# A fixed order for TensorE in the RWKV scans: small products grouped by shape in each hop, three units of the output projection moved to the end

## Chip, cores and metric

The kernel runs on one core of a Trainium2 chip. The metric is the device time of one execution in microseconds; it is compared as the median of several runs.

## The reference

One layer of a hybrid backbone over 640 tokens (512 latent, 128 context) of 2048 channels: RMS norm with adaLN modulation, an input projection, a bidirectional RWKV-7 time mixing of 16 heads on one half of the channels and a gated MLP on the other, an output projection, then a SwiGLU channel mixer and a last norm. The change touches the RWKV scan and the output projection behind it:

```python
def _delta_scan(r, w, k, v, aa, bb, s0, reverse):
    def step(S, inp):
        r_t, w_t, k_t, v_t, a_t, b_t = inp
        sa = jnp.einsum('bhvk,bhk->bhv', S, a_t)
        S = S * w_t[:, :, None, :] + sa[..., None] * b_t[:, :, None, :] + v_t[..., None] * k_t[:, :, None, :]
        return S, jnp.einsum('bhvk,bhk->bhv', S, r_t)
    s_fin, ys = lax.scan(step, s0, xs, reverse=reverse)
...
    for d in range(2):
        ...
        y, s_fin = _delta_scan(rh, decay, kd, vh, -kk, kk * heads(a),
                               s0[:, d].astype(F32), reverse=(d == 1))
        out = out + _group_norm(y, lp['gn_w'], lp['gn_b']) \
            + jnp.sum(rh * kd * lp['r_k'], axis=-1, keepdims=True) * vh
    o = (out.reshape(B, T, D_A) * gate).astype(dtype)
...
    x = x + g1 * (jnp.concatenate([o_a, o_b], axis=-1) @ lp['w_out'])
```

The scans run over the context alone from a zero state (its last state is an output) and over the latent tokens from a given state, in both directions.

## The kernel before

The 640 tokens are cut into ten chunks of 64: eight latent (`LATC`), two of context (`CTXC`). Sixteen heads make eight pairs (`NPAIR`); a pair holds its two heads in the two halves of the 128 partitions, and both directions d side by side. An earlier stage has worked out for each pair, direction and chunk a record of 576 columns (`REC`) and stored it in device memory (`d_S`); the scan stage loads them (`load_next`, L1041 to L1047, one record for both directions, eight buffers).

The scan stage begins at L1014. `recur(p)` (L1062) runs two chains of one pair: latent, eight steps, and context, two steps. A step has three phases, and the generator gives the word back after each:

- **w**: four products w_ps = (part of the record) x (state ST), 64 rows by 64 columns (L1117); VectorE adds a part of the record to make W (L1122). In the same phase `outputs` writes what the step before left over: y_ps is the sum of four 64x64 products with the old state (`states`, L1083) and four of 128 rows by 64 columns (`chunk`, L1088); ScalarE copies it to Y with its row sums (L1102), and the next record is loaded.
- **u**: four 64x64 products u_ps (L1132), copied back into the record by VectorE (L1135) and ScalarE (L1136).
- **s**: VectorE scales the old state to SG (L1150), four 128x64 products s_ps (L1153), and VectorE makes the new state SN = s_ps x decay + SG (L1159; L1157 where there is no old state). SN is the ST of the next step.

`swap` (L1053) transposes the states at the beginning and the end of a pair, again with four 64x64 products. All these operands are plain 32-bit floats, and each such product shows as two records in the trace.

When a pair has been through its steps, `finish(p)` (L1167) norms Y: GpSimd subtracts the means (L1182), ScalarE squares (L1186), VectorE sums (L1187), GpSimd takes the root (in the helper at L132) and multiplies (L1192), each once per direction. Then 64x64 products with unit matrices add the two directions (pO, L1200, the "join"), VectorE adds the bonus term (L1204), two products of 128x320 make each half of the gate (pmm, L496), VectorE multiplies (L1208), and the result goes to d_o.

Meanwhile `wout_b` (L1215) does the half of the output projection that does not depend on the scans: for two groups q of four 128-row blocks and 16 column blocks m, a unit `wout(m, q)` (L990) of two halves with four triples each: three products of 128x128 by 320 columns (L999, L1000, L1001). Its weights are loaded and split in two parts (L162 to L164), and VectorE adds each half to x1T (L1012). For q = 0 the columns of x are transposed first (pxT, L1232) and copied by ScalarE (L1233). The other half of the projection, which needs the scans' results, follows behind the stage (L1382 to L1384).

The order of the work: a loop of 117 hops (`hops`, L1247) advances each running pair by one phase; a new pair starts every 13 hops (`OFF`) and runs 26 hops, so two are under way most of the time. After each pair's phase the Mixer m3 issues some of `wout_b` by a budget (L1257), and after each hop the Mixer m2 some of `finish`. Before the loop, m3 runs eight units of the 32. Within this program order the framework's scheduler sets the order of each engine's queue by priority and its own estimate of when operands are ready; the queues are fixed when the program is compiled. PSUM has eight banks: two for w_ps, s_ps and swap, one for u_ps, two for y_ps, one shared by pO, pmm and pxT, two for the units of the projection.

Of the kernel before, what the change touches and what calls it, by code (L numbers as in the profile page):

```python
# [10 lines left out]
F32 = mybir.dt.float32  # L11
# [44 lines left out]
WTAIL = 8  # L56
OFF = 13
MB = 6
# [26 lines left out]
def flow_step(ctx: ExitStack, tc, x_prompt, x_sample, state_rwkv, c, c_ctx, w_mod, b_mod,  # L85
# [929 lines left out]
    with ExitStack() as ph:  # L1015
        rw = ph.enter_context(tc.tile_pool(name="rw", bufs=1))
        sm = ph.enter_context(tc.tile_pool(name="sm", bufs=2))
        pws = ph.enter_context(tc.tile_pool(name="pws", bufs=2, space=PSUM))
        pu = ph.enter_context(tc.tile_pool(name="pu", bufs=1, space=PSUM))
# [32 lines left out]

        def swap(src):  # L1053
            ps = pws.tile([P, 2, CH], F32, tag="ws", name="swap")
            for d in range(2):
                for h in range(2):
                    TE.matmul(ps[hsl(h), d, :], src[hsl(h), d, :], I2[hsl(h), :], start=True, stop=True)
            o = sm.tile([P, 2, CH], F32, tag="ST", name="ST", bufs=7)
            V.tensor_copy(o, ps)
            return o  # L1060

        def recur(p):  # L1062
# [7 lines left out]
            yield 1  # L1070
            late = []

            def outputs():
                if not late:
                    return


                ys = [py.tile([P, 2, CH], F32, tag=f"y{d}", name="y_ps") for d in range(2)]

                def states(e, r, ST, **kw):  # L1080
                    for d in range(2):
                        for h in range(2):
                            TE.matmul(ys[d][hsl(h), e, :], r[hsl(h), d, F_R + CH:F_R + P], ST[hsl(h), d, :], **kw)  # L1083

                def chunk(e, r, **kw):
                    for d in range(2):
                        for h in range(2):
                            TE.matmul(ys[d][hsl(h), e, :], r[:, d, F_G + CH * h:F_G + CH * h + CH],  # L1088
                                      r[:, d, F_Z + CH * h:F_Z + CH * h + CH], **kw)

                for e, (cc, r, ST) in enumerate(late):
                    if ST is None:
                        chunk(e, r, start=True, stop=True)
                    elif e == 0:
                        states(e, r, ST, start=True, stop=False)
                        chunk(e, r, start=False, stop=True)
                    else:
                        chunk(e, r, start=True, stop=False)
                        states(e, r, ST, start=False, stop=True)
                for e, (cc, r, ST) in enumerate(late):  # L1100
                    for d in range(2):
                        S.activation(u.Y[:, d, cc[d], :], ys[d][:, e, :], AF.Copy, accum_out=u.ys[:, d, cc[d]:cc[d] + 1])  # L1102
                    load_next()
                late.clear()

            for step in range(len(LATC)):
                act = [c for c in chains if step < len(seqs[c[0]])]
                Ws = []
                for ctx_, ST in act:
                    r = recs[p, ctx_, step]  # L1110
# [3 lines left out]
                    w_ps = pws.tile([P, 2, CH], F32, tag="ws", name="w_ps")  # L1114
                    for d in range(2):
                        for h in range(2):
                            TE.matmul(w_ps[osl(h), d, :], r[hsl(h), d, F_R:F_R + CH], ST[hsl(h), d, :],  # L1117
                                      start=True, stop=True)
                    W = sm.tile([P, 2, CH], F32, tag="W", name="W", bufs=4)
                    for h in range(2):  # L1120
                        q = osl(h)
                        V.tensor_add(W[q], w_ps[q], r[q, :, F_Z + CH * h:F_Z + CH * h + CH])  # L1122
                    Ws.append(W)
                outputs()
                yield 1
                for (ctx_, ST), W in zip(act, Ws):
                    r = recs[p, ctx_, step]
                    ups = pu.tile([P, 2, CH], F32, tag="u", name="u_ps")
                    for d in range(2):
                        for h in range(2):  # L1130
                            q = osl(h)
                            TE.matmul(ups[q, d, :], r[q, d, F_T:F_T + CH],  # L1132
                                      r[q, d, F_Z + CH * h:F_Z + CH * h + CH] if W is None else W[q, d, :],
                                      start=True, stop=True)
                    V.tensor_copy(r[0:64, :, F_Z + CH:F_Z + P], ups[0:64])  # L1135
                    S.copy(r[64:128, :, F_Z:F_Z + CH], ups[64:128])  # L1136
                yield 1
                for ch in act:
                    ctx_, ST = ch
                    cc = seqs[ctx_][step]  # L1140
                    r = recs.pop((p, ctx_, step))
                    late.append((cc, r, ST))
                    if step + 1 == len(seqs[ctx_]) and not ctx_:
                        continue
                    s_ps = pws.tile([P, 2, CH], F32, tag="ws", name="s_ps")
                    SN = sm.tile([P, 2, CH], F32, tag="ST", name="SN", bufs=7)
                    ge = gend[:, p].rearrange("p d c -> p (d c)")[:, flip(cc)].unsqueeze(2)
                    if ST is not None:
                        SG = sm.tile([P, 2, CH], F32, tag="SG", name="SG", bufs=4)
                        V.tensor_tensor(out=SG, in0=ST, in1=ge.to_broadcast([P, 2, CH]), op=ALU.mult)  # L1150
                    for d in range(2):
                        for h in range(2):
                            TE.matmul(s_ps[hsl(h), d, :], r[:, d, F_X + CH * h:F_X + CH * h + CH],  # L1153
                                      r[:, d, F_Z + CH * h:F_Z + CH * h + CH], start=True, stop=True)
                    for d in range(2):
                        if ST is None:
                            V.tensor_scalar_mul(SN[:, d, :], s_ps[:, d, :], ge[:, d])  # L1157
# [756 lines left out]
```

## Time and profile before

| | |
|---|---|
| median of three runs | 3405.29 us (3395.33 to 3405.65) |
| the profiled execution | 3410.02 us |
| its span | 3408.2 us |
| granted TensorE clock, mean | 0.97 |
| first w_ps of the scan | 1242.1 us |
| last copy of y_ps | 1537.8 us |

The times in the views are microseconds from the beginning of the span. PE is TensorE's products, DVE VectorE, ACT ScalarE, POOL GpSimd, SP the engine that issues most transfers. A row of the table of windows has the stretch, its length, then for each engine the busy time and the number of instructions (PE, weight loads, DVE, ACT, POOL), the granted clock, the share of the transfer engines and GB/s. A row of the groups has line, engine, operation, output and inputs, shape and number, then the busy time in us and the mean of one in ns, then the idle time ahead of it and what ended it. A row of the timeline has the start, the time until the last one ends, engine, line and number; products are pipelined, so the distance of starts is what a product holds of the queue, and its own time is longer.

### The profile page before, as it was taken

How to read it: one execution, taken by the hardware profiler on the slowest of the kernel's cores; microseconds unless marked ns; L12 is line 12 of the kernel's file. 1: busy time of each engine (PE TensorE's matmuls, PEld its weight loads, DVE VectorE, ACT ScalarE, POOL GpSimd, SP SyncE). 2: the span in 40 equal slices, each digit the busy share in tenths (PEclk: the TensorE clock that was granted, in tenths of full speed). 3: DMA queues.
4: the chain of work that ended last, by engine and by line, in shares of the span. 5: the costliest groups of instructions: out<-in, count | busy, mean ns of one | idle time of the engine just before them, and what ended most of it. 6: DMA issues, size and time to landing. Idle time of an engine off the chain costs nothing.

```text
span 3408.2 us, 72541 instructions
## 1 busy us (share of the span) xinstructions
PE 3249.5 (95%) x28216; PEld 2934.2 (86%) x28216; DVE 2411.4 (71%) x4320; ACT 1450.7 (43%) x3161; POOL 1263.0 (37%) x1112
## 2 busy tenths in 40 slices
PE   6899999999999999998899999999999999999996
PEld 3688777777877887777889999999999999999996
DVE  4547666756866766664887777777777787877787
ACT  3334443433434434333564444444444445443365
POOL 0001122111212103322336565656656555555543
PEclk8999999889999999999999999999999999999998
DMA  8766776566677677654543434344343455543553
GB/s 321 233 188 185 184 189 170 154 171 179 186 186 180 170 226 231 209 163 145 173 124 103 130 114 122 114 126 122 111 123 121 129 165 165 158 138 115 154 163 115
DMA packets 736208, 550.11 MB, mean 161 GB/s; under 512 B 140360, under 2 KB 670040, under 8 KB 727032
## 3 DMA queue, kind: packets, MB, share of 16 engines
q1 hardware_dynamic: 723544, 531.78, 52.5%
q0 software_dynamic: 9984, 13.13, 1.8%
q8 instruction: 222, 3.64, 0.4%
q14 instruction: 122, 1.00, 0.1%
q10 hardware_dynamic: 2336, 0.57, 0.1%
HBM read 436.68 MB, written 111.28 MB: 161 GB/s over the span
## 4 chain that ended last, share of the span: by engine, by line
PE 76%; DVE 11%; issue 4%; DMA 4%; POOL 2%; ACT 2%; SPq 0%; DVEq 0%; ACTq 0%; POOLq 0%
PE P L1529 15%; PE P L1527 14%; PE P L1528 14%; PE big L185 4%; PE big L187 4%; PE big L186 4%; PE pG L624 3%; PE pm L869 2%; PE big L999 2%; DMA raw<-in_w_in_dram 1%; DVE lo L1330 1%; DMA wt<-in_w_mod_dram 1%; PE big L1382 1%; PE big L1384 1%; PE pmm L496 1%
## 5 line engine op out<-in xcount | busy, mean ns | idle before, releaser
L1529 PE MATMUL P<-xo,lo 128*128 128x320 f32 x2352 | 728.1, 310 | 2.3 <-DVE lo L1330 2.2
L1527 PE MATMUL P<-xo,hi 128*128 128x320 f32 x2352 | 727.8, 309 | 1.8 <-ACT hi L1329 1.8
L1528 PE MATMUL P<-xo,hi 128*128 128x320 f32 x2352 | 727.7, 309 | 0.0
L1330 DVE TENSOR_TENSOR lo<-raw,hi 128x512 fp32r<-128x512 f32 x532 | 502.7, 948 | 179.1 <-ACT hi L1329 174.3
L1329 ACT CAST hi<-raw 128x512 fp32r<-128x512 f32 x532 | 330.7, 622 | 496.5 <-PE P L1528 395.1
L185 PE MATMUL big<-h_hi,hi 128*128 128x320 f32 x1376 | 458.2, 333 | 7.8 <-ACT h_hi L341 4.0
L1529 PEld LDWEIGHTS P<-xo,lo 128*128 128x128 f32 x2352 | 442.5, 188 | 3.0 <-DVE lo L1330 3.0
L187 PE MATMUL big<-h_hi,lo 128*128 128x320 f32 x1376 | 444.2, 323 | 0.7 <-DVE lo L164 0.7
L186 PE MATMUL big<-h_lo,hi 128*128 128x320 f32 x1376 | 443.7, 322 | 0.9 <-DVE h_lo L342 0.9
L1527 PEld LDWEIGHTS P<-xo,hi 128*128 128x128 f32 x2352 | 442.7, 188 | 2.0 <-ACT hi L1329 2.0
L1528 PEld LDWEIGHTS P<-xo,hi 128*128 128x128 f32 x2352 | 442.5, 188 | 0.0
L1440 POOL TENSOR_TENSOR raw<-raw 128x512 f32<-128x512 f32 x252 | 407.6, 1627 | 14.9 <-DVE lo L1330 3.3
L1529 PE MATMUL P<-xd,lo 128*128 128x320 f32 x1232 | 383.3, 311 | 14.1 <-DVE lo L1330 13.7
L1527 PE MATMUL P<-xd,hi 128*128 128x320 f32 x1232 | 381.8, 310 | 4.2 <-ACT hi L1329 1.9
L1528 PE MATMUL P<-xd,hi 128*128 128x320 f32 x1232 | 380.7, 309 | 0.0
L164 DVE TENSOR_TENSOR lo<-raw,hi 128x512 fp32r<-128x512 f32 x268 | 185.7, 695 | 243.1 <-ACT hi L163 217.7
L185 PEld LDWEIGHTS big<-h_hi,hi 128*128 128x128 f32 x1376 | 268.4, 195 | 84.0 <-issue 56.9
L163 ACT CAST hi<-raw 128x512 fp32r<-128x512 f32 x268 | 165.4, 619 | 292.4 <-PE big L186 143.1
L186 PEld LDWEIGHTS big<-h_lo,hi 128*128 128x128 f32 x1376 | 268.6, 195 | 17.4 <-issue 11.8
L187 PEld LDWEIGHTS big<-h_hi,lo 128*128 128x128 f32 x1376 | 268.2, 195 | 12.2 <-issue 4.8
L1329 ACT CAST hi<-rawd 128x512 fp32r<-128x512 f32 (+1 forms) x288 | 168.9, 588 | 244.6 <-PE P L1528 207.7
L1529 PEld LDWEIGHTS P<-xd,lo 128*128 128x128 f32 x1232 | 231.2, 188 | 20.4 <-DVE lo L1330 20.3
(362 smaller groups left out, 6303.3 us busy)
## 6 DMA issues: line engine op xcount, KB each, us to landing
wt<-in_w_mod_dram SPq DMA_DIRECT2D x96, 1024.0 KB
raw<-in_w_ffn_gate_dram SPq DMA_DIRECT2D x182, 256.0 KB
raw<-in_w_ffn_up_dram SPq DMA_DIRECT2D x182, 256.0 KB
rec<-d_S SPq DMA_DIRECT2D x80, 576.0 KB
raw<-in_w_in_dram SPq DMA_DIRECT2D x172, 256.0 KB
rawd<-in_w_ffn_down_dram SPq DMA_DIRECT2D x128, 256.0 KB
raw<-in_w_out_dram SPq DMA_DIRECT2D x96, 256.0 KB
xd<-d_os SPq DMA_DIRECT2D x66, 320.0 KB
```

The lines of the kernel that those rows point to most:

```text
L163: S.copy(hi, raw)
L164: V.tensor_sub(lo, raw, hi.bitcast(F32))
L185: TE.matmul(halves[hf], hi[:, k, :], h_hi[:, kb, s], start=(kb == 0), stop=False)
L186: TE.matmul(halves[hf], hi[:, k, :], h_lo[:, kb, s], start=False, stop=False)
L187: TE.matmul(halves[hf], lo[:, k, :], h_hi[:, kb, s], start=False, stop=(kb == KB - 1))
L624: TE.matmul(two[h][:, cc - c0, :], X[s, cc, :, :].rearrange("p s t -> p (s t)"), R[s, cc, :, :].rearrange("p s t -> p (s t)"), start=True, ...
L1329: S.copy(hi[:, 0:nk], raw[:, 0:nk])
L1330: V.tensor_sub(lo[:, 0:nk], raw[:, 0:nk], hi[:, 0:nk].bitcast(F32))
L1440: G.tensor_tensor(out=o[:, 0:nk], in0=p[:, 0:nk], in1=q[:, 0:nk], op=ALU.subtract)
L1527: TE.matmul(ps, hi[:, k, :], xk[:, 0, :], start=f, stop=False)
L1528: TE.matmul(ps, hi[:, k, :], xk[:, 1, :], start=False, stop=False)
L1529: TE.matmul(ps, lo[:, k, :], xk[:, 0, :], start=False, stop=l)
```

## The change

TensorE's queue gets the order of the program inside the hop loop, by a guard around it. Each hop is written in two halves: in the first all running pairs issue their 64x64 products (w, states, u, swap, and the joins of a finished pair), in the second their 128x64 products (outputs, s), then come the gates of a finished pair and one run of the projection. `recur` gives the word back six times a step instead of three. Both chains of a pair share one bank for w_ps, u_ps or s_ps; these and swap have four banks together, y_ps has one. SG is made in the phase of u. `finish` is cut into `norm` (one step per hop, from the hop after the pair's end), `join` and `gate` (the halves of each in the hops that follow, two hops later). Two units of the projection instead of eight run ahead of the loop, and three are kept back until it has ended. A unit's transposes of x stand inside the unit, behind its first and third triple, instead of ahead of it.

```diff
-WTAIL = 8
+FRONT = 2
+REST = 3
+LATE = 2
...
-        pws = ph.enter_context(tc.tile_pool(name="pws", bufs=2, space=PSUM))
-        pu = ph.enter_context(tc.tile_pool(name="pu", bufs=1, space=PSUM))
+        pws = ph.enter_context(tc.tile_pool(name="pws", bufs=4, space=PSUM))
...
             for step in range(len(LATC)):
                 act = [c for c in chains if step < len(seqs[c[0]])]
-                Ws = []
-                for ctx_, ST in act:
-                    r = recs[p, ctx_, step]
+                rs = [recs[p, ctx_, step] for ctx_, ST in act]
+                w_ps, Ws = bank("w_ps"), []
+                for e, ((ctx_, ST), r) in enumerate(zip(act, rs)):
+                    if ST is not None:
+                        for d in range(2):
+                            for h in range(2):
+                                TE.matmul(w_ps[osl(h), e, d, :], r[hsl(h), d, F_R:F_R + CH], ST[hsl(h), d, :],
+                                          start=True, stop=True)
...
-                outputs()
-                yield 1
+                ys = states()
+                yield
+                outputs(ys)
+                yield
+                ups = bank("u_ps")
...
+                SG, ge = [], []
...
+                yield
+                yield
+                yield
+                s_ps, go = bank("s_ps"), []
...
-        m3.add(wout_b(), 8.0 + 16 * 7.2)
-        m3.run(4.0 + 8 * 4.0)
+        m3 = Mixer()
+        m3.add(wout_b(), 8.0 + 16 * 6.4)
+        m3.run(4.0 + FRONT * 3.2)
...
-                m3.run(m3.left / max(1, 2 * (hops - hop - WTAIL)))
-            m2.run(m2.left / MB)
+        with tc.manual_schedule(engines={mybir.EngineType.PE}):
+            for hop in range(hops):
+                if hop == OFF * nxt and nxt < NPAIR:
+                    act.append((nxt, recur(nxt)))
+                    nxt += 1
+                for p, gen in act:
+                    next(gen)
+                for job in list(after):
+                    if job[0] < 0:
+                        next(job[2], None)
+                    elif job[0] in (LATE, LATE + 1):
+                        join(job[1], job[0] - LATE)
+                for p, gen in list(act):
+                    if next(gen, 0) == 0:
+                        act.remove((p, gen))
+                        after.append([-7, p, norm(p)])
+                for job in list(after):
+                    if job[0] in (LATE + 2, LATE + 3):
+                        gate(job[1], job[0] - LATE - 2)
+                    job[0] += 1
+                    if job[0] > LATE + 3:
+                        after.remove(job)
+                m3.run(max(0.0, m3.left - REST * 3.2) / (hops - hop))
         assert not act
+        (_, p, gen), = after
+        for _ in gen:
+            pass
+        for i in range(2):
+            join(p, i)
+        for hf in range(2):
+            gate(p, hf)
         m3.drain()
```

More of the change, by code (lines that the diff above doesn't have):

```diff
@@ L1074, in outputs @@
+            def outputs(ys):
                 if not late:
                     return
-                ys = [py.tile([P, 2, CH], F32, tag=f"y{d}", name="y_ps") for d in range(2)]
-                def states(e, r, ST, **kw):
+                for e, (cc, r, ST) in enumerate(late):
                     for d in range(2):
                         for h in range(2):
[L1083 to L1099, printed above, removed]
+                            TE.matmul(ys[hsl(h), e, d, :], r[:, d, F_G + CH * h:F_G + CH * h + CH],
+                                      r[:, d, F_Z + CH * h:F_Z + CH * h + CH], start=False, stop=True,
+                                      skip_group_check=True)
@@ new lines, in gate @@
+        def gate(p, hf):
+            u = U[p]
+            s = slice(HALF * hf, HALF * hf + HALF)
+            ps = po.tile([P, HALF], F32, tag="g", name="pmm")
+            for i, (l, r) in enumerate(((u.g2a, gs1), (u.g2b, gs2))):
+                TE.matmul(ps, l, r[:, s], start=(i == 0), stop=(i == 1))
+            V.scalar_tensor_tensor(out=u.bv[:, s], in0=u.bv[:, s], scalar=gb2[:, p:p + 1],
+                                   in1=ps, op0=ALU.add, op1=ALU.mult)
+            if hf:
+                nc.sync.dma_start(d_o[p], u.bv)
+                dump(f"o{p}", u.bv)
```

168 lines of the change are left out of this document (81 added, 87 removed).

## The prediction

> **What bounds the kernel now.** First the page's first lines, then the table of windows over the scan stage, where all of the edit lies.
>
> ```profile
> span 3408.2 us, 72541 instructions
> PE 3249.5 (95%) x28216; PEld 2934.2 (86%) x28216; DVE 2411.4 (71%) x4320; ACT 1450.7 (43%) x3161; POOL 1263.0 (37%) x1112
> 1240.00:1540.00 300.00, 299.56 (x4384) 227.61 (x4384) 194.15 (x637) 102.76 (x481) 76.38 (x102) 1.00 0.66 200
> 1363.20:1479.00 115.80, 115.73 (x1687) 87.34 (x1686) 75.08 (x246) 37.06 (x176) 31.35 (x42) 1.00 0.68 207
> 1545.00:1550.00 5.00, 1.25 (x18) 1.07 (x20) 0.00 (x0) 0.72 (x1) 4.52 (x6) 0.54 0.23 92
> 1550.00:1555.00 5.00, 4.36 (x70) 4.05 (x67) 1.61 (x3) 0.00 (x0) 0.00 (x0) 0.50 0.02 3
> ```
>
> From 1240 to 1540 TensorE is never without a product in flight; VectorE is at 65%, ScalarE at 34%, the transfers at 0.66. So the stage lasts as long as TensorE's queue takes. Just behind it lie 10 us in which TensorE is nearly idle or at half its clock (0.54 and 0.50). The third window is three pair periods exactly: the swaps of four pairs lie in it,
>
> ```profile
> L1057 PE MATMUL swap<-I,s x32: 218/218/267, 1363.2 to 1479.3; 64*64 64x64 f32 x32
> ```
>
> so a pair (13 hops) takes 115.8/3 = 38.6 us. Next the groups by line and form in that window, and a few us of the timeline in order of time, to see what fills it.
>
> ```profile
> L999 PE MATMUL big<-oh,hi 128*128 128x320 f32 x82 | 33.6, 409 | 0.0
> L1000 PE MATMUL big<-ol,hi 128*128 128x320 f32 x82 | 25.7, 313 | 0.0
> ...
> 1400.20 0.27 PE L1117 MATMUL w_ps<-SN,rec 64*64 64x64 f32 x2
> 1400.22 0.27 PE L1083 MATMUL y_ps<-SN,rec 64*64 64x64 f32 x2
> 1400.60 0.45 PE L1088 MATMUL y_ps<-rec 128*64 128x64 f32 x8
> 1400.98 0.42 PE L999 MATMUL big<-oh,hi 128*128 128x320 f32 x1
> ...
> 1402.64 0.45 PE L1132 MATMUL u_ps<-W,rec 64*64 64x64 f32 x8
> 1403.02 0.42 PE L999 MATMUL big<-oh,hi 128*128 128x320 f32 x1
> 1403.15 0.27 DVE L1135 COPY rec<-u_ps 64x128 f32<-64x128 f32 x1
> 1403.28 0.31 PE L1000 MATMUL big<-ol,hi 128*128 128x320 f32 x1
> 1403.42 0.31 PE L1001 MATMUL big<-oh,lo 128*128 128x320 f32 x1
> 1403.54 0.28 DVE L1150 TENSOR_TENSOR SG<-ST,gend 128x128 f32<-128x128 f32 x1
> 1403.66 0.45 PE L1117 MATMUL w_ps<-ST,rec 64*64 64x64 f32 x8
> ...
> 1531.97 0.33 PE L1200 MATMUL pO<-I,Y 64*64 64x64 f32 x4
> 1532.09 0.33 PE L1200 MATMUL pO<-J,Y 64*64 64x64 f32 x4
> 1532.88 0.45 PE L1153 MATMUL s_ps<-rec 128*64 128x64 f32 x8
> 1533.49 0.27 PE L1200 MATMUL pO<-J,Y 64*64 64x64 f32 x1
> ```
>
> Inside a run a wide product starts 0.145 us after the last (1403.28 to 1403.42) and small ones 0.029 apart (four in 0.115). But three wide ones alone hold 0.64 (1403.02 to 1403.66), not 0.435: 0.205 for the change of shape. Eight records (four products) of 64x64 alone hold 0.38 (1402.64 to 1403.02) for 0.235 of work; of 128x64 also 0.38, sixteen of them 0.61 (1532.88 to 1533.49). A first wide product shows as 0.42 instead of 0.31, and the mean of L999, 409, is almost that of a first one: nearly each of the 82 triples opens a run of its own. About 27 runs of wide products per pair, 2 per hop, each with its switches, are what the change attacks. The Trainium skill, TensorEngine Tiling, section Key Properties, says that changing the tiling mode drains the array; the 0.145 to 0.205 lost per switch agree. If that rule failed and the gaps were waits for data, grouping would return none of them.
>
> **The change part by part.**
>
> Fixed order. In two successive halves of a hop all 64x64 products stand together, then all 128x64, then the wide run, of which the budget is 90.4/0.4/117 = 1.93 triples per hop (four reloads of o take a little of it: 1.85). Two pairs run 13 hops apart, one phase of three apart, so hops repeat in three kinds. Kind 1: w and old states of one pair; outputs of it and s of the other. Kind 2: u of one, w and states of the other; outputs. Kind 3: u; s. From the rows, 64x64: 0.40 for w with states (sixteen records from 1400.20 to 1400.60: the two fill different quarters of the array and overlap), 0.40 + 0.235 = 0.64 with u ahead, 0.38; 128x64: 0.61, 0.38, 0.38. A third of 13 hops of each kind: 64x64 (0.40 + 0.64 + 0.38) x 4.33 = 6.2; 128x64 1.37 x 4.33 = 5.9. Wide: 24 triples x 0.435 + 13 x 0.205 = 13.1. Added once per pair, inside runs that exist: joins 80 records x 0.029 = 2.3, two swaps 0.5, the context chain's two steps 1.6; and two gates,
>
> ```profile
> 1434.67 1.47 PE pmm L496 x4
> 1290.58 0.59 PE pxT L1232 x4
> ```
>
> 1.47 less a switch, 1.27 each: 2.5. Sum 32.1 us for a pair instead of 38.6. Of the 6.5, 1.5 are 3.4 triples which go elsewhere; 5.0 are switches no longer made.
>
> The scan: seven such periods 225; the transposes of 14 units (0.59 and a fifth one, 0.7 each) 10; 13 hops of the first pair alone: wide 13.1, 64x64 (0.40 + 0.38) x 4.33 = 3.4, 128x64 (0.38 + 0.38) x 4.33 = 3.3, swap and context 2, in all 22; of the last, without the context but with joins 2.3 and gates 2.5 of the one before, 25. Together 282 us.
>
> Stalls in it. Now each wait stops everything: behind the waiting product stand the hop's other products and its wide run, and for them VectorE's sums and ScalarE's copies. The tightest step is s to the next w, with only a wide run between them (0.205 + 6 x 0.145 = 1.07 us).
>
> ```profile
> 1404.68 0.45 PE L1153 MATMUL s_ps<-rec 128*64 128x64 f32 x8
> 1405.18 0.47 DVE L1159 SCALAR_TENSOR_TENSOR SN<-s_ps,gend,SG 128x64 f32<-128x64 f32 x2 [0.41 <-PE s_ps L1153]
> ...
> L1012 DVE SCALAR_TENSOR_TENSOR x1T<-big,modc,x1T 128x256 f32<-128x256 f32 x50 | 23.9, 477 | 7.7 <-PE big L1001 3.9 <-ACT x1T L1233 2.4 <-DMA x1T<-in_x_sample_dram 1.1
> L164 DVE TENSOR_TENSOR lo<-raw,hi 128x512 fp32r<-128x512 f32 x25 | 16.9, 677 | 0.0
> ```
>
> SN starts 0.50 after s and takes 0.47. In kind 3 VectorE copies u (0.51 after it, 0.27) 0.51 to 0.78 into the hop, makes SG (0.28) until 1.08 and SN until 1.55; w is due at 0.38 + 0.38 + 1.07 = 1.83. Margin 0.28 us; one sum of 0.477 or split of 0.677 ahead eats it, and in hops of one triple (1.40) it is gone. I take 0.3 us for each three hops, 12 us; bounds 0, and 0.9 (both in the way) x 39 = 35.
>
> Grouping both chains in one PSUM bank, SG made a hop earlier and four shared banks instead of two and one cost nothing: same instructions, one tile read within a hop, four hold two hops. Loading the next record moves half a hop later, with eight buffers for 10 records in 13 hops. Without that cover it would be a wait at each w; that is a rival. The norm of a pair becomes one step per hop, 10.8 us of GpSimd (the tail below) inside eight hops of 2.5 us; else the joins stand first in the queue and block it.
>
> Two units ahead instead of eight. Before, the scan's first w is at 1242.1, behind eight units of wide products.
>
> ```profile
> L1117 PE MATMUL w_ps<-ST,rec x64: 218/218/267, 1242.1 to 1481.3; 64*64 64x64 f32 x64
> 1210.85 1.48 SPq L1051 DMA_DIRECT2D s<-in_state_rwkv_dram  x2
> 1221.32 1.38 PE L738 MATMUL psp<-wspT,vt 128*128 128x128 f32 x10 [0.75 <-DVE vt L725]
> ```
>
> Now it can start once the states have come (issued until 1212.3, so 1213 at best), or, if the previous stage's last products (psp) come first in the queue, at 1223. I take 1217, between the two. The six units moved are in the 282.
>
> Three units last. The tail before, from the chain of waits:
>
> ```profile
> 1538.35 1.40 POOL Y L1182 x2
> 1549.14 2.41 PE pO L1200 x38
> 1552.18 2.45 PE pO L1200 x40
> 1559.25 0.56 DVE bv L1208
> ```
>
> The last pair's norm runs 10.8 us on GpSimd (1538.35 to 1549.14) with little on TensorE; 72 wide products, 10.5 us, now lie under it. Without that cover they would cost their 10.5. TensorE kept busy does the joins in 1.2 us, not 2.4 at half clock: 2.5 off, some 3 with the gate products; bounds 0 and 5.
>
> **Sum.** The scan before ends where the last norm begins, at 1538. After: 1217 + 282 + 12 = 1511, 27 earlier; with the tail's 3, 30 in all. The profiled execution took 3410.0 (span 3408.2 and 1.8 around it): 3380. The median shown, 3405.3, is 4.7 lower; so 3375.
>
> **Rivals.** (A) Slower: VectorE's queue in lock step. A wide unit's half ends every fourth triple, 54 times. Its two sums wait for the end of a wide run; if they stand in VectorE's strict queue ahead of SN, w waits for 0.477 + 0.276 + 0.47 + 0.1 = 1.3 us each time, 70 us, less 12 counted: 3375 + 58 = 3433. It decides from 30/54 = 0.56 us per half. For it: VectorE at 65% would rise to about 70%. Against it: such sums already run between SN and SG without showing as idle time of TensorE.
>
> (B) Records late.
>
> ```profile
> DMA packets 43183, 59.94 MB, mean 200 GB/s; under 512 B 5884, under 2 KB 22911, under 8 KB 43135
> rec<-d_S SPq DMA_DIRECT2D x72, 576.0 KB
> ...
> 1340.00:1360.00 20.00, 19.92 (x379) 15.46 (x378) 13.31 (x45) 7.88 (x43) 2.97 (x6) 1.00 0.85 272
> ```
>
> Were 200 GB/s all that this mixture reaches, 60 MB and six units with their columns (3.5 MB) would take 318 us: end at 1535, total 3402, no change. Against it: the share is 0.66 here, and 1340 to 1360 moved 272 GB/s at 0.85.
>
> (C) Half the gain. w and states overlap now because they alternate in time (1400.20, 1400.22); written one after the other they may not: 0.2 us x 72 = 14, and the start at 1223 adds 6: 3395. The Trainium skill, TensorE: Matmul & The Clock Gate, in its step-by-step section, says that products stay in program order and only weight loads are pulled ahead; taken strictly that would make this loss certain. The order in the old queue is not visible, so the trace does not decide.
>
> (D) The order changes nothing, because the extra 0.145 to 0.205 are not switches: then only the tail's 3 remain, 3402; it goes with B.
>
> **How the numbers follow.** Forecast 0.63 (own range 3357, with no stalls, a start at 1213 and 5 in the tail, to 3398, with stalls at their worst), A 0.14, B with D 0.10, C 0.13. A measurement here tells some 0.3%, 10 us, from no change. Faster by more: 0.63 and 0.05 of C, 0.68; within: the rest of C and B, 0.17; slower: A and a little of B, 0.15. The range takes in B and C, leaves out most of A, and goes 7 us below the best ends, since the unit prices come from few rows: 3350 to 3412.
>
> **What would show it.** Right: swaps about 33 us apart; the mean of L999 near 365 in the scan, as about half the triples open a run; first w before 1225; no low clock between norm and joins; 72 wide products under the norm. Wrong: idle of TensorE ahead of w_ps put down to SN (A) or to records (B), first w behind 1235, or sixteen records of w and states holding 0.6 us (C).

## The result and the profile after

| | before | after |
|---|---|---|
| median | 3405.29 us (3395.33 to 3417.14, 5 runs) | 3371.73 us (3367.86 to 3384.01, 5 runs) |
| ratio of the runs | | 0.9919, 95% interval 0.9898 to 0.9941 |
| profiled execution | 3410.02 us | 3370.27 us |

The kernel is 20 to 35 us faster (0.0059 and 0.0102 of 3405). The page's first lines, after:

```profile
span 3368.5 us, 72526 instructions
PE 3199.5 (95%) x28216; PEld 2912.7 (86%) x28216; DVE 2431.8 (72%) x4328; ACT 1449.9 (43%) x3161; POOL 1262.4 (37%) x1112
```

The same number of products keeps TensorE busy for 50 us less. Not all of that belongs to the edit. Two landmarks enclose it: the last product of the input projection (the last start of big<-h_hi,lo), behind which the stages touch, and the first product of the channel mixer (the FFN; the first start of C). The view of one tile gives first and last start; first before, then after with the landmarks of the scan between them:

```profile
L187 PE MATMUL big<-h_hi,lo x1376: 303/308/635, 53.3 to 1202.0; 128*128 128x320 f32 x197
...
L1459 PE MATMUL C<-xo,hi x128: 305/309/468, 1690.8 to 1752.9; 128*128 128x320 f32 x128
```

```profile
L188 PE MATMUL big<-h_hi,lo x1376: 303/308/636, 54.8 to 1183.7; 128*128 128x320 f32 x197
...
L1112 PE MATMUL w_ps<-ST,rec x64: 218/218/267, 1213.2 to 1431.9; 64*64 64x64 f32 x64
...
L1095 PE MATMUL y_ps<-rec x640: 222/222/271, 1218.9 to 1488.0; 128*64 128x64 f32 x160
...
L1495 PE MATMUL C<-xo,hi x128: 306/309/468, 1649.1 to 1711.6; 128*128 128x320 f32 x128
```

The projection ended 18.3 us earlier (1202.0 against 1183.7), ahead of every line that the change touches and with TensorE's products in the same order. Between the landmarks lie 488.8 us before and 465.4 after: 23.4 us. The table of windows shows one of the stretches in which the 18 us arose, first before, then after:

```profile
620.00:660.00 40.00, 38.62 (x369) 32.76 (x369) 27.62 (x71) 17.74 (x40) 6.88 (x12) 0.70 0.65 176
```

```profile
620.00:660.00 40.00, 39.41 (x580) 31.48 (x578) 34.04 (x80) 20.05 (x42) 4.82 (x9) 0.89 0.67 191
```

The granted clock was 0.70 there instead of 0.89, and from 556 to 620 us 0.87 instead of 0.99. (The 369 and 580 products that started there are not the same ones.) Product by product, the second profile is 1.3 us ahead at 548 us of the first, 13.4 at 636, 21.0 at 752 and 18.3 at the projection's end. So the comparison below goes by **stretches**, from the projection's end to the first w ("front"), from there to the last y_ps product ("scan"), and from there to the FFN ("tail"), of one profile of each kernel. Where a kernel was profiled twice, the sums agree within 0.3 us (before) and 1.9 us (after). Each ratio is to runs of the kernel before that were made beside it; their medians lie between 3398.62 and 3405.29.

| | projection's end | to first w | scan | to the FFN | sum | median, ratio to before |
|---|---|---|---|---|---|---|
| before | 1202.0 | 40.1 | 295.3 | 153.4 | 488.8 | 3405.29 |
| before2 | 1182.1 | 40.2 | 295.2 | 153.1 | 488.5 | one run, 3390.72 |
| after | 1183.7 | 29.5 | 274.8 | 161.1 | 465.4 | 3371.73, 0.9919 (0.9898 to 0.9941) |
| after2 | 1183.2 | 31.8 | 275.8 | 159.7 | 467.3 | 3373.66, 0.9923 (0.9894 to 0.9952) |
| split_run | 1189.6 | 31.9 | 302.9 | 159.8 | 494.6 | 3402.25, 0.9992 (0.9971 to 1.0013) |
| every2 | 1187.4 | 21.1 | 309.9 | 157.6 | 488.6 | 3400.87, 0.9979 (0.9963 to 0.9996) |
| no_guard | 1192.4 | 21.3 | 290.8 | 159.8 | 471.9 | 3380.03, 0.9950 (0.9929 to 0.9971) |
| before_guard | 1192.4 | 40.2 | 319.7 | 157.1 | 517.0 | 3429.00, 1.0076 (1.0052 to 1.0100) |
| front8 | 1177.8 | 57.3 | 256.5 | 157.8 | 471.6 | 3385.13, 0.9958 (0.9940 to 0.9975) |
| front5_tail | 1194.9 | 44.1 | 272.1 | 154.9 | 471.1 | 3379.06, 0.9935 (0.9917 to 0.9952) |
| tail_order | 1193.0 | 31.6 | 275.5 | 155.1 | 462.2 | 3372.15, 0.9899 (0.9874 to 0.9924) |
| rest0 | 1192.3 | 32.4 | 285.5 | 154.7 | 472.6 | 3381.86, 0.9945 (0.9922 to 0.9967) |
| po_first | 1187.8 | 25.5 | 277.6 | 160.5 | 463.6 | 3370.48, 0.9897 (0.9870 to 0.9925) |
| po_first_tail4 | 1201.2 | 24.5 | 272.0 | 154.7 | 451.2 | 3366.10, 0.9886 (0.9856 to 0.9915) |

The change gained in the front (10.6 us) and in the scan (20.5), and lost in the tail (7.7). From the FFN's first product to the end of the span it is 1717.4 us before (3408.2 - 1690.8) and 1719.4 after (3368.5 - 1649.1), nothing gained. The 22 us of the stretches (the mean of two profiles each: 488.6 and 466.4) lie in the interval of 20 to 35, near its lower end; whether the medians hold a few us more than that is not settled by these profiles.

Inside the scan, the profile after: the window from the swap of one pair to that of the third pair after it, the swaps in it, the first wide line in this window and in the whole scan, and what TensorE waited for in the whole scan (us in total, times, the longest):

```profile
1333.40:1429.80 96.40, 95.00 (x1664) 77.81 (x1654) 73.36 (x241) 36.84 (x177) 33.37 (x43) 1.00 0.79 248
```

```profile
L1060 PE MATMUL swap<-I,s x32: 218/218/218, 1333.4 to 1429.8; 64*64 64x64 f32 x32
```

```profile
L1000 PE MATMUL big<-oh,hi 128*128 128x320 f32 x65 | 23.6, 363 | 0.0
...
L1000 PE MATMUL big<-oh,hi 128*128 128x320 f32 x212 | 77.8, 367 | 0.0
```

```profile
PE w_ps L1112 <- DVE SN L1167: 1.1, 2, 0.6
...
PE u_ps L1132 <- DVE W L1121: 0.5, 2, 0.4
...
```

A pair takes 96.4/3 = 32.1 us instead of 38.6, with 65/3 = 21.7 triples instead of 82/3 = 27. The mean of the first wide line fell from 409 to 363 ns between the two windows, and from 401 to 367 over the scans: after, 122 of the 212 triples open a run. All waits of the scan together are 3.2 us, of which 1.1 us for SN. Next a piece of the timeline, a hop that transposes states besides:

```profile
1396.59 0.27 PE L1112 MATMUL w_ps<-SN,rec 64*64 64x64 f32 x2
1396.62 0.27 PE L1085 MATMUL y_ps<-SN,rec 64*64 64x64 f32 x2
1396.69 0.23 PE L1112 MATMUL w_ps<-SN,rec 64*64 64x64 f32 x2
1396.72 0.22 PE L1085 MATMUL y_ps<-SN,rec 64*64 64x64 f32 x2
...
1396.90 0.40 PE L1060 MATMUL swap<-I,s 64*64 64x64 f32 x8
...
1397.61 0.42 PE L1000 MATMUL big<-oh,hi 128*128 128x320 f32 x1
...
1398.68 0.27 PE L1132 MATMUL u_ps<-W,rec 64*64 64x64 f32 x2
```

The compiled queue holds the four w products first and the four of the old state behind them, as the new code writes them. In time they alternate, and all sixteen records hold 0.31 us (1396.59 to 1396.90): two sets that fill different quarters of the array still overlap.

### The profile page after: what moved, and what is told of

Its sections match the earlier page's. It is cut to its first block, busy times and chain, and to the rows that moved or that the text cites. A ratio compares the mean times of both kernels' runs of the same rounds, so it can differ in the third digit from the quotient of the medians.

```text
span 3368.5 us, 72526 instructions
## 1 busy us (share of the span) xinstructions
PE 3199.5 (95%) x28216; PEld 2912.7 (86%) x28216; DVE 2431.8 (72%) x4328; ACT 1449.9 (43%) x3161; POOL 1262.4 (37%) x1112
## 4 chain that ended last, share of the span: by engine, by line
PE 72%; DVE 12%; issue 6%; DMA 4%; POOL 3%; ACT 2%; DVEq 0%; SPq 0%; POOLq 0%; ACTq 0%
PE P L1565 15%; PE P L1563 14%; PE P L1564 14%; PE big L186 4%; PE big L188 4%; PE big L187 4%; PE pG L625 2%; PE pm L870 2%; DVE mx L770 1%; DVE lo L1366 1%; DMA wt<-in_w_mod_dram 1%; PE big L1000 1%; PE big L1418 1%; PE big L1419 1%; PE big L1420 1%
## 5 line engine op out<-in xcount | busy, mean ns | idle before, releaser
L1366 DVE TENSOR_TENSOR lo<-raw,hi 128x512 fp32r<-128x512 f32 x532 | 511.2, 964 | 171.0 <-ACT hi L1365 165.8
L165 DVE TENSOR_TENSOR lo<-raw,hi 128x512 fp32r<-128x512 f32 x268 | 186.5, 698 | 234.1 <-ACT hi L164 218.3
L1565 PEld LDWEIGHTS P<-xd,lo 128*128 128x128 f32 x1232 | 231.9, 188 | 21.2 <-DVE lo L1366 21.2
```

Source lines behind the costliest of these rows:

```text
L165: V.tensor_sub(lo, raw, hi.bitcast(F32))
L1366: V.tensor_sub(lo[:, 0:nk], raw[:, 0:nk], hi[:, 0:nk].bitcast(F32))
L1565: TE.matmul(ps, lo[:, k, :], xk[:, 0, :], start=False, stop=l)
```

## The experiments

"Theory" is the prediction's: what fell is the price of the changes of shape. Diffs are against the changed kernel unless said otherwise. Stretches and sums are those of the table above.

### The change again, the price of a switch, and the cover of the wide run

`after2` is the changed kernel again. `split_run` cuts each wide run in two, one part between the two halves of the hop; `every2` makes a double run in every second hop.

```diff
 split_run
+                share = max(0.0, m3.left - REST * 3.2) / (hops - hop) / 2
+                m3.run(share)
                 for p, gen in list(act):
...
-                m3.run(max(0.0, m3.left - REST * 3.2) / (hops - hop))
+                m3.run(share)
 every2
-                m3.run(max(0.0, m3.left - REST * 3.2) / (hops - hop))
+                if hop % 2 or hop == hops - 1:
+                    m3.run(2 * max(0.0, m3.left - REST * 3.2) / (hops - hop))
```

> The changed kernel once more, to tell what of the first pair of profiles was the change and what the execution. The stretch that holds the whole edit, from the last product of the input projection to the first of the FFN's first blocks, was 488.8 us before (1202.0 to 1690.8) and 465.4 after (1183.7 to 1649.1); the 18.3 us by which the projection itself ended earlier lie in code that is the same. If that is so, this run has the stretch at 465 within 3 us, and the end of the projection anywhere between 1180 and 1205. If the change itself moved the earlier stage, the projection ends at 1184 again.

> The changed kernel with each hop's wide run cut in two, one part between the 64x64 and the 128x64 products. Its queue has 195 wide runs in the scan instead of 122. Theory (each change of shape costs its 0.2 us): 73 x 0.205 = 15 us more, the stretch at 480. Rival (the extra time of a first product is a wait for data, which a break only shows): the stretch stays at 465 or gets shorter, since the waits get more cover.

> The changed kernel with a double wide run every second hop: 80 wide runs instead of 122. Switches alone: 42 x 0.205 = 9 us less, the stretch at 456. The theory has a price for the cover too: in each hop without a wide run the next w or u stands some 0.4 to 0.8 us after its input's source, so it waits for VectorE, some 58 x 0.5 = 29 us: the stretch at 485. If the margins that I worked out were too tight, nearer 456.

`after2` agrees with the first profile within 2 us in each part but the front (2.3). Its projection ends at 1183.2, which fits both of its expectations; before2, below, tells them apart. In split_run the groups by form and the waits over the scan say:

```profile
L1000 PE MATMUL big<-oh,hi 128*128 128x320 f32 x213 | 86.6, 406 | 0.0
```

```profile
PE pmm L1226 <- DVE bv L1227: 3.4, 1, 3.4
PE w_ps L1112 <- DVE SN L1167: 2.2, 5, 0.6
```

About the same number of triples, 213 for 212, but the mean of the first line is back at 406 and the scan 27.6 us longer than the mean of the change's two. One long wait is 3.4 of that and SN 1.1 more; the queue has 73 more wide runs (195 for 122), which leaves (27.6 - 4.5)/73 = 0.32 us each, above the 0.205 of the prediction and well above zero. Part of that is the clock: behind the long wait TensorE ran at half clock,

```profile
1382.00:1386.00 4.00, 3.33 (x6) 1.60 (x7) 1.30 (x4) 0.26 (x1) 0.00 (x0) 0.50 0.08 23
1386.00:1390.00 4.00, 4.00 (x39) 3.10 (x38) 0.53 (x3) 0.52 (x4) 0.21 (x1) 0.50 0.29 102
```

and at 0.74 from 1390 to 1394. At full clock these 12 us would have been some 5 shorter (8 x 0.50 + 4 x 0.26), an estimate; it leaves (27.6 - 4.5 - 5.0)/73 = 0.25 us for each run. What the rest above 0.205 is was not taken apart. That the gaps are waits which grouping cannot return (the prediction's D) is refuted: cutting the runs alone takes back the whole gain, 0.9992.

In every2 there are fewer runs still, 80, and the scan is longest of the three. Its waits over the scan:

```profile
PE u_ps L1132 <- DVE W L1121: 8.9, 12, 1.3
PE w_ps L1112 <- DVE SN L1167: 8.5, 20, 0.6
PE s_ps L1159 <- ACT rec L1137: 3.2, 5, 0.9
```

20.6 us of waits for VectorE and ScalarE: the sum of 488.6 is near the 485 of the expectation that put a price on the cover. The 1.07 us of wide products at the end of each hop are the cover under which W, SN and the copies are made; a hop without them waits. So of the three lengths tried, one run per hop is the best at this budget.

### The guard alone, the grouping alone

`no_guard` keeps the grouped program and leaves the order of the queue to the scheduler; `before_guard` gives the kernel before a fixed order without grouping. In the second, each half of a pair's join is issued in one piece.

```diff
 no_guard
-        with tc.manual_schedule(engines={mybir.EngineType.PE}):
+        with ExitStack():
 before_guard (against the kernel before)
+        with tc.manual_schedule(engines={mybir.EngineType.PE}):
             for hop in range(hops):
...
-                    yield 0.4
...
-                yield 0.8
+                yield 2.8
```

> The changed program without the fixed order: the scheduler arranges TensorE's queue again, which then has 133 wide runs, 143 of 64x64 and 121 of 128x64 in the scan, where the changed kernel has 122, 109 and 92 and the one before 197, 194 and 132. Theory (the price is per switch, whoever sets the order): 11 x 0.205 + 34 x 0.145 + 29 x 0.15 = 11.5 us over the changed kernel's stretch of 466 (mean of 465.4 and 467.4), so 478. Rival (the fixed order as such brings the gain): back near 489. Rival (fixed order costs stalls that the scheduler avoids): 466 or less.

> The kernel before with its hop loop under the fixed order, nothing grouped (a join issued in one piece, which the order needs): 176 wide runs, 163 of 64x64, 118 of 128x64 instead of 197, 194 and 132. Theory: 21 x 0.205 + 31 x 0.145 + 14 x 0.15 = 11 us fewer switches, but nothing now stands between a product and the one that needs its result, so stalls give it back: the stretch at 489 or longer. Rival (a fixed order as such is better): 470.

Without the guard 17 of the 22 us remain (471.9 against 488.6), between the 478 of the theory and the 466 of the second rival. The order in which the program is written, its PSUM banks and its budgets, which no run takes apart, together already make the scheduler group: 133 wide runs instead of 122, and a mean of L1000 as low:

```profile
L1000 PE MATMUL big<-oh,hi 128*128 128x320 f32 x222 | 80.5, 362 | 0.0
```

With the guard alone, the scan is 24 us longer than before. Its two largest waits over the scan:

```profile
PE u_ps L1132 <- ACT rec L1136: 11.0, 16, 0.7
...
PE pmm L496 <- DVE bv L1207: 6.6, 6, 1.2
```

All waits of that scan are 22.3 us, and the granted clock was 0.54 from 1480.0 to 1487.5 and from 1524.0 to 1539.0, which by estimate costs another 10 (22.5 x 0.46). A fixed order is no gain in itself; where the order written stops short of covering a wait, it costs. On top of the grouping it pays 5 us in the sum (471.9 against 466.4; the ratios, 0.9950 and 0.9923, have intervals that overlap, so the total does not show it): the scan is 15.5 us shorter than without the guard, the front 9.3 longer.

### The tail: what stands under the last norm

`tail_order` carries the guard to the end of the stage, with the kept units ahead of the last joins. `rest0` keeps no unit back.

```diff
 tail_order
-        assert not act
-        (_, p, gen), = after
-        for _ in gen:
-            pass
+            assert not act
+            (_, p, gen), = after
+            for _ in gen:
+                pass
+            m3.drain()
...
-        m3.drain()
 rest0
-REST = 3
+REST = 0
```

> The changed kernel with the end under the fixed order too: the three units kept back stand whole ahead of the last joins. After, two join products stand ahead of most of them in the queue and wait 4.3 us for GpSimd, and the clock falls to half. Theory: that wait goes, the stretch is 4 to 6 us shorter, 460. Rival (the end hangs on the last norm, joins, gates and the reload of their result whatever stands ahead): 465.

> The changed kernel with no unit kept back for the end (REST = 0); three more units run inside the scan. A unit costs 3.05 us of scan (from front8), so the scan should be 284 instead of 275 us by every theory. Theory (the kept units bring almost nothing as they stand: in the queue a product of pO stands ahead of 50 of the 72, and 33 run behind the last gate): from the last copy of y_ps to the first product of the FFN 153 us, as in the kernel before, instead of 160 to 161; from the projection's end to the FFN 467 to 470 us against 465 to 467. Rival (the prediction's step: the 72 products and the clock behind them are worth some 13 us under the last norm): that stretch stays 160 us or more, and the whole is 475 to 480 us, the total some 10 us above the change.

What TensorE waited for in the tail, first after, then tail_order:

```profile
PE pO L1214 <- POOL Y L1201: 5.4, 2, 4.3
PE big L1418 <- ACT oh L987: 1.7, 2, 1.2
```

```profile
PE big L1000 <- DVE x1T L1013: 1.7, 1, 1.7
PE pmm L1226 <- DVE bv L1217: 1.0, 1, 1.0
```

Outside the guard the scheduler placed a single join product ahead of 56 of the 72 wide ones; it waits 4.3 us for GpSimd's norm and everything waits with it, and a second one another 1.1. 33 wide products stand behind the last gate, 33 x 0.145 = 4.8 us. The windows after show what follows, the clock that the prediction wanted gone:

```profile
1496.00:1500.00 4.00, 2.95 (x14) 2.48 (x16) 1.28 (x3) 0.62 (x1) 3.75 (x5) 0.52 0.03 6
1500.00:1505.00 5.00, 5.00 (x84) 4.62 (x83) 0.91 (x3) 0.00 (x0) 0.81 (x1) 0.70 0.18 52
```

With the products really under the norm (tail_order) the granted clock is 1.00 from the last y_ps product at 1500.1 to 1524, and the stretch to the FFN is 155.1, 4.6 and 6.0 less; the sum, 462.2, is nearer the theory's 460 than the rival's 465. It is still no shorter than before: the wide products, with 1.7 us of waiting among them, end 13.7 us behind the last y_ps product, while in the kernel before the joins went on at 11.7. rest0 falls between its two expectations: scan 285.5 and tail 154.7 as the theory had it, but the sum 472.6 is 2.6 above the theory's band and 2.4 below the rival's. By these profiles the kept units are worth some 6 us as the change places them (472.6 less 466.4) and 10 where tail_order puts them (472.6 less 462.2).

### The front: more units ahead

`front8` runs eight units ahead of the loop, `front5_tail` five, with tail_order's end.

```diff
 front8
-FRONT = 2
+FRONT = 8
 front5_tail (against tail_order)
-FRONT = 2
+FRONT = 5
```

> The changed kernel with eight units ahead of the scan again instead of two. In its trace TensorE waits some 12 us between the projection and the first w (5.4 for ScalarE ahead of psp, 3.2 for a load, 3.1 for the states ahead of the swap), which the two units do not fill. Theory: six more units fill it, and the scan gets shorter by their 25 us while the front grows by 13: the stretch at 455. Rival (as I forecast: the move brings a start 25 us earlier and is part of the gain): 470 or more. It may lose a little where hops with fewer wide products cover less.

> Five units ahead and the end under the fixed order (the three units kept back whole ahead of the last joins). If both waits are real and separate, the stretch is 10 (front) and 4 (end, as measured: 462.2 against 466.4) shorter than the changed kernel's 466: 452, and the time some 14 us under its 3372. If five units do not fill the front, 457; if the end hides the front's gain, 462.

Both missed the theory: 471.6 instead of 455 and 471.1 instead of 452. front8 came out as its rival has it, 470 or more; front5_tail lies above all three numbers of its expectation. Six units make the front 27.8 us longer than in the first profile of the change, 4.6 each, and the scan only 18.3 shorter, 3.05 each. The front still waits, whatever the number of units: 13.3 us after, 13.8 in front8. The waits in the front, first before, then after:

```profile
PE psp L738 <- DVE vt L725: 0.7, 1, 0.7
PE pw L694 <- DMA wsp<-in_w_spatial_dram: 0.6, 1, 0.6
```

```profile
PE psp L739 <- ACT gq L681: 5.4, 1, 5.4
PE pw L695 <- DMA wsp<-in_w_spatial_dram: 3.2, 1, 3.2
PE swap L1060 <- DMA s<-in_state_rwkv_dram: 3.1, 1, 3.1
PE pxT L1252 <- ACT x1T L1253: 1.0, 2, 0.7
PE pxT L1252 <- DVE sp L740: 0.6, 1, 0.6
```

The last row is the clue: a transpose of x waits for VectorE's sp, which reads psp, a tile of the stage before. The pools of PSUM are laid out in the order in which they are opened; with four banks for w_ps, u_ps, s_ps and swap opened first, the pool of pxT lands on a bank which psp still holds. The compiled programs show it: pxT shares a bank with psp in the changed kernel, and not in the kernel before nor in po_first, below. So the scheduler puts all units but the first behind psp, and nothing fills the waits for wsp, s and gq. In the kernel before, its eight units were spread among them. Two runs show what the second unit costs behind psp: in every2 and no_guard it stands behind the first w, and w starts 21.1 and 21.3 us after the projection's end instead of 29.5. The waits cost more than their length here, for the granted clock is low as well; two windows of the front after, then the whole front of po_first_tail4 (below), which hardly waits:

```profile
1190.00:1200.00 10.00, 1.83 (x14) 1.22 (x14) 4.14 (x9) 2.49 (x5) 1.19 (x1) 0.62 0.92 313
1200.00:1213.20 13.20, 9.37 (x55) 8.37 (x55) 8.10 (x18) 3.40 (x7) 0.00 (x0) 0.77 0.69 219
```

```profile
1201.20:1225.70 24.50, 22.38 (x162) 20.67 (x161) 17.58 (x39) 10.12 (x21) 1.73 (x2) 1.00 0.89 291
```

### The bank of pxT

```diff
 po_first
-        pws = ph.enter_context(tc.tile_pool(name="pws", bufs=4, space=PSUM))
         po = ph.enter_context(tc.tile_pool(name="po", bufs=1, space=PSUM))
+        pws = ph.enter_context(tc.tile_pool(name="pws", bufs=4, space=PSUM))
 po_first_tail4: the same with tail_order's end, and
-FRONT = 2
+FRONT = 4
```

> The changed kernel with the PSUM pool of pO, pmm and pxT opened ahead of the four banks of w_ps, u_ps, s_ps and swap, nothing else. Measured from the projection's last product, the first w stood at 29.5 and 31.8 us in the two runs of the change, with TensorE waiting some 12 us between (for wsp, for s, for gq, for sp and x1T). Theory (pxT shares its bank with psp, so that the units ahead cannot fill these waits): with another bank the second unit's products stand ahead of psp; psp still starts some 18.4 us after the projection's end, w 4 us later, at 22 to 24; the scan stays 275; from the projection's end to the first product of the FFN 458 us instead of 465 to 467, some 8 us off the total. Rival (the front is bound by its own chain of loads and ScalarE, and the wide products only move): first w at 29 to 32, 465 to 467, no change.

> The pool order of po_first, the end of the stage under the guard with the rest of the projection ahead of the last joins as in tail_order, and four units ahead of the loop instead of two. Theory: the two further units fill the waits ahead of psp, so first w at 24 to 26 us after the projection's end although 42 more wide products stand ahead; the scan loses two units of 3.05 us, 269; the tail is that of tail_order (132 from the last gate to the FFN); from the projection's end to the FFN 446 to 450 us instead of 465 to 467, total some 17 us below the change, near 3355. Rival (every unit ahead costs what it costs in front8, 4.6 us against 3.05 in the scan): 463 to 466, total no better than tail_order's 3372.

The waits in the front, po_first and then po_first_tail4:

```profile
PE psp L739 <- ACT gq L681: 7.7, 1, 7.7
PE pw L695 <- DMA wsp<-in_w_spatial_dram: 0.8, 1, 0.8
PE swap L1060 <- DVE sp L740: 0.6, 1, 0.6
```

```profile
PE psp L739 <- DVE vt L726: 1.4, 1, 1.4
PE pw L695 <- DMA wsp<-in_w_spatial_dram: 0.7, 1, 0.7
```

Two lines exchanged, and the second unit moves ahead of psp: the waits for s and x1T are gone, the one of 0.6 us for sp now stands ahead of swap, that for wsp falls from 3.2 to 0.8. What is left, 7.7 us for gq, wants more products than two units have, so the front is 25.5, above the 22 to 24 expected, and the sum 463.6 instead of 458: 2.8 us below the change's mean, a third of the 8 expected. Four units fill it: 48 more wide products ahead than in po_first and yet a front of 24.5 (24 to 26 expected), a sum of 451.2 against 446 to 450, and 463 to 466 by the rival. This accounts for most of the misses above: front5_tail, with one unit more and the old order of the pools, needs 471.1, some 5 of it for two spells of low clock in its scan (0.66 from 1257 to 1262, 0.57 from 1363 to 1371).

po_first_tail4 has the shortest stretches, 15 us below the change and 37 below the kernel before. Its median, 3366.10, missed the 3355 expected; its projection ended at 1201.2 in the profile, and six runs lie between 3356.31 and 3376.20. Its ratio, 0.9886 (0.9856 to 0.9915), overlaps that of the change, 0.9919 (0.9898 to 0.9941): the total alone doesn't separate the two.

### The kernel before once more

> The kernel before once more, for its profile. If the 18 us between the two first profiles ahead of the edit (projection's end at 1202.0 before, 1183.7 after, in the same order of instructions) come from the clock granted in that execution, the projection ends somewhere between 1178 and 1202 here too, as in the other profiles, and the stretch from there to the first product of the FFN is 487 to 491 us again. If it belongs to the kernel, the projection ends within 2 us of 1202.

```profile
L187 PE MATMUL big<-h_hi,lo x1376: 303/308/636, 54.1 to 1182.1; 128*128 128x320 f32 x197
...
L1459 PE MATMUL C<-xo,hi x128: 305/309/415, 1670.6 to 1731.5; 128*128 128x320 f32 x128
...
620.00:660.00 40.00, 39.40 (x525) 31.80 (x524) 34.02 (x79) 20.65 (x44) 5.11 (x8) 0.90 0.59 170
```

Same kernel, projection's end at 1182.1 instead of 1202.0, clock 0.90 instead of 0.70 in that window, and 488.5 us to the FFN again. So the 18 us between the first two profiles are not the edit's. Beside after2, whose projection ends at 1183.2, the profiled runs differ by 3390.72 - 3369.73 = 21.0 us, nearly the same as the stretches (21.2).

## Why the prediction was right, step by step

The forecast, 3375 us of 3350 to 3412, was 3 us from the median, and "faster" was right. Its three terms (front, scan, tail) were not: errors in them offset each other. By the stretches it had -25, -2 and -3, in all -30; measured are -9.5, -20 and +7, in all -22 (means of two profiles each, from the table). That the time came out so near is luck: the same median less 22 would be 3383, and the few us by which the medians lie further apart than the stretches are not explained.

- **The price of a change of shape, and the pair's period.** Right: 32.1 us forecast, 96.4/3 = 32.1 measured, and a mean of L1000 of 367 against "near 365". That the two agree to a tenth is partly luck: the three periods of the window are 30.4, 33.1 and 32.7 us by the first records of their swaps, the three ahead of it 28.2, 34.6 and 34.8. The period had a few parts that offset: 21.7 triples a pair instead of 24, 1.0 us less, and 1.4/3 = 0.5 us of idle time in the window. A run of six wide products takes the 1.07 us worked out (in the timeline of the same window 1397.61 to the next small product at 1398.68). That it is the cut into runs and not a wait is shown by split_run.
- **The scan, 282 us and 12 of stalls.** Mis-sized: 274.8 and 275.8. The first pair alone took 22.6 us, from the first w to the next pair's swap at 1235.8 (22 forecast). The waits are 3.2 us instead of 12, and the transposes hold the queue for 6 us instead of 10; they now stand inside wide runs which are there anyhow. The rest, some 6 us, is spread over unit prices and a smaller number of triples; the lower bound of 282, "no stalls", was too high.
- **The tightest step.** Right as a mechanism, too dear in size: w waits for SN 1.1 us in all (0.3 us for each three hops were taken). It comes back where the cover is gone, in every2: 8.5 us for SN, 8.9 for W.
- **First w at 1217.** This step failed. It set the start by the states' arrival, 11 to 21 us behind the projection's end; it was 29.5 and 31.8 us behind it. That 1213.2 looks like the forecast's own lower bound is the 18 us of another clock ahead; on the clock of the first profile it would be 1231.5 to 1233.8, hardly short of the 1235 named as the sign of failure. What was overlooked: the eight units were the filling of the waits of the last stage's tail, and the new order of the PSUM pools keeps the second unit's transposes out of it (po_first, po_first_tail4). So that unit and the loop's first wide run stand between psp and w; without them w starts at 21 (every2, no_guard), the later of the two ends between which 1217 was chosen. The clock of 0.62 and 0.77 in these waits was not counted either. "Four shared banks instead of two and one cost nothing" was true of the scan and false ahead of it.
- **Three units last, -3.** This step failed: +7.7 and +6.3. The wide products were to lie under the norm; outside the guard the scheduler's queue put a waiting join ahead of most. The low clock between norm and joins stayed (0.52 and 0.70). With the queue in the order assumed (tail_order) the stretch is 155.1, still 1.7 above before: the 10.5 us are hidden for the most part, as the prediction counted, but of the 2.5 and 0.5 behind them nothing is seen, since the wide products outlast the norm by some 2 us (13.7 against 11.7).
- **Rival A, VectorE in lock step**: did not come about. VectorE is busy for 73.36 of 96.4 us, 76%, more than the 70% which the rival assumed, yet TensorE waits 1.1 us for SN.
- **Rivals B and D**: no wait of the scan is put down to the load of a record, while the transfers moved 248 GB/s at a share of 0.79, above the 200 of B; D fell with split_run.
- **Rival C, the overlap lost**: refuted for the overlap, by the timeline above; its late start (1223, 21 behind the projection) was surpassed. The Trainium skill, TensorE: Matmul & The Clock Gate, in its step-by-step section, says that products stay in program order. The records here do not agree: a y_ps product starts at 1396.62, ahead of w_ps products (1396.69) that stand before it in the queue. They agree with the Trainium skill, TensorEngine Tiling (Array Packing), Key Properties, by which tiles work independently. The prediction was right to leave the strict rule as a rival only.

## What to carry to other kernels

Group small products by shape when TensorE's queue is the bound, with one run of wide products in each round long enough to cover the other engines' answers: fewer, longer runs lose again, and a fixed order without such a cover is slower than the scheduler's. When work is taken away ahead of a stage, ask which waits it was filling, and look at the order in which PSUM pools are opened, since a tile of the next stage on a bank still held keeps that stage's work from filling them. Compare two profiles from landmark to landmark, not by their ends, and carry a hand-made order to the end of the work that it is meant to arrange.

## What the hardware showed unexpectedly

Products of 64x64 in different quarters start out of the order of the queue: four of w_ps and four of y_ps, written one set after the other, alternate with 0.03 us between starts. A wait can cost twice: in split_run one of 3.4 us was followed by 8 us at a granted clock of 0.50 and 4 at 0.74, some 5 us more. And the clock granted in the stages ahead of the scan differs from one execution to the next of the same kernel: 0.70 and 0.90 in the window 620 to 660, and the projection ends at 1202.0 and 1182.1; over the fourteen profiles, which share the order of TensorE's products up to there, between 1177.8 and 1202.0. What sets the grant was not tried.
